# A fused decoder layer: the transfers that keep u's low half, and one more pair by seven products

## The chip, the cores and the metric

The kernel runs on one core of a Trainium2 chip. A core has five engines with an instruction queue each, every queue strictly in order: TensorE (PE, matrix products into PSUM banks), VectorE (DVE), ScalarE (ACT), GpSimd (POOL) and SyncE (SP). ACT, POOL and SP also issue DMA transfers, in the order in which they stand in their queues. The metric is the device time of one execution in microseconds (us).

## The reference, cut to what matters

One decoder layer on 256 tokens of width 2048, in fp32. The attention half (two head groups of eight heads) is not touched. The second half is

```python
h = rmsnorm(x, norm_mlp_pre)
u = square(relu(h @ w_up))            # w_up 2048 x 8192
x = x + rmsnorm(u @ w_down, norm_mlp_post)   # w_down 8192 x 2048
```

## The kernel before, in words

**Products.** A fp32 number is split in two rounded halves, hi = round(a) and lo = a - hi. A product then is three matmuls into one PSUM bank (hi by hi, hi by lo, lo by hi; line 296, called by `three`). A weight tile of 128 rows by 1024 columns (`raw`) is loaded by SP, ACT rounds it to `hi` (line 306, or 310 with a row gain) and DVE subtracts to get `lo` (307 or 311). There are five `raw` buffers and eight of `hi` and `lo`; ACT and DVE may work up to six tiles ahead of PE.

**Seven products.** Two weight tiles and two 128-row blocks of the left operand form a 2 by 2 block product, which eight products do plainly. For some pairs it is done by seven (Strassen's way, `seven_products`): 21 matmuls for 24. Such a pair is loaded by one POOL DMA of 1024 KB (line 374); DVE makes the sums `t` and `u` of weights (lines 361, 365, 366), and half a tile and three whole ones are split in place of two. Extra sums are gathered in four more banks `m` and added at the end (`close`, lines 1052 and 1055, and 1121).

**Up projection.** Eight chunks j of 1024 columns. Chunks 2 to 5 do rows 8 to 15 tile by tile (8 tiles) and rows 0 to 7 as four pairs by seven. The pairs are loaded by turns into the buffers `ab` and `ab2`; the profile and the queue listings print `ab2` as `ab` too, the listings with a number (`ab_3503`). A buffer may be loaded again once DVE has made the last `lo` from it. At a chunk's end DVE adds the extra sums (1121), ACT makes relu with the row scale (937, tile `r`), PE transposes `r` (line 300, tile `rt`), and ACT squares that into u (949). The first transposes of a chunk stand among the matmuls of the next chunk, and PE can pass nothing that waits. Between the first and the second `r`, ACT's queue holds a `hi<-u` that needs the next chunk's first weight sums.

**u's low half.** u has 16 pieces g of 128 by 1024, two per chunk. Its low half is made by DMAs rather than by DVE (`lo_away`): for each 512-column half ACT writes minus the rounded u into a tile `neg` (line 960; it shares the two buffers of tag `r`), ACT's queue sends it to `ukeep` in DRAM (962), and a POOL DMA with an addition adds u to it (964), for which POOL's queue waits until the first transfer has landed. The down projection loads the result back as `ulo` (976), and ACT makes `uhi` (975).

**Down projection.** Two halves c of 1024 output columns, each over 16 pieces g, that is 32 pairs kp, of which `DOWN_SEVEN` lists those by seven. Left sums of u for a pair are made and split by DVE and ACT (989 to 991, tile `s`). For a pair in both lists the first half stores `s` in DRAM (983, on SP) and the second half loads it (404, on POOL).

**What sets the order.** The program is laid down once, by a planner with a clock of its own (`Flow`). Each matmul moves the clock by 0.216 planned us. Side work is a generator: `flow.start(gen, d)` starts it d planned us later, `yield d` puts its next step d planned us on, and a step's instructions are appended to their engines' queues at that point. Weight tiles are emitted when PE's plan is within the look-ahead.

Of the kernel before, what the change touches and what calls it, by code (L numbers as in the profile page):

```python
# [101 lines left out]
def up_steps(first, *groups):  # L102
    steps = [("k", k) for k in first]
    for i, ks in enumerate(groups):
# [9 lines left out]
N_SEVEN = [sum(w == "w" for w, _ in steps) for steps in UP_STEPS]  # L114


DOWN_SEVEN = ((5, 7, 9, 11, 15, 17, 19, 21, 25, 27, 29), range(3, 28, 2))
SHARED = [k for k in DOWN_SEVEN[0] if k in DOWN_SEVEN[1]]
GT = FF // 512
DOWN_STEPS = [[s for kp in range(2 * GT)  # L120
               for s in ([("w", kp)] if kp in ws else [("k", 2 * kp), ("k", 2 * kp + 1)])] for ws in DOWN_SEVEN]

# [141 lines left out]
def layer(nc, tc, io):  # L264
    flow = Flow()
# [12 lines left out]
    def bank(i, name):  # L278
        return ps.tile([P, 512], F32, tag=f"bank{i}", bufs=1, name=name)
# [19 lines left out]
    def transpose(out, a):  # L299
        nc.tensor.transpose(out, a, ident)  # L300
        flow.spend(TR)
# [128 lines left out]
    def seven_down(c, kp):  # L430
        def load():

            n = DOWN_SEVEN[c].index(kp)
            raw = dpl["ab"]
# [498 lines left out]
    def up_evac(j, b, i, acc, order):  # L933

        yield UP_STEP * order
        r = late["up"].tile([P, 512], F32, tag="r", bufs=2, name=f"r{j}_{b}")
        nc.scalar.activation(r, acc, AF.Relu, scale=rstd2[b])
        yield D_UP if j > 1 else 2 * D_UP
        t = bank(i, f"rt{j}_{b}")
        for k in range(4):  # L940
            transpose(t[:, k * P:(k + 1) * P], r[:, k * P:(k + 1) * P])
        if j not in uT:
            if j in (0, 1, 10, 11, 12, 13):
                t2 = late["u01" if j < 2 else "ab2" if j < 12 else "ab"][:, j % 2 * CW:(j % 2 + 1) * CW]
            else:
                tag = {"tag": "T", "bufs": 2} if j > 13 else {}
                t2 = late["up"].tile([P, CW], F32, name=f"uT{j}", **tag)
            uT[j] = t2.rearrange("p (k s) -> p k s", k=4)
        nc.scalar.activation(uT[j][:, :, b * P:(b + 1) * P], t.rearrange("p (k s) -> p k s", k=4), AF.Square)
        if b and j:  # L950
            flow.start(lo_away(j), 5.0 + 7.0 * (j % 2))

    def lo_away(g):

        ukeep[g] = dram.tile([P, CW], F32, name=f"ukeep{g}")
        u = uT[g].rearrange("p k s -> p (k s)")
        for h in range(2):
            c = slice(h * 512, (h + 1) * 512)
            t = late["up"].tile([P, 512], F32, tag="r", bufs=2, name=f"neg{g}_{h}")
            nc.scalar.activation(t.bitcast(F32R), u[:, c], AF.Copy, scale=-1.0)  # L960
            yield 1.0
            nc.scalar.dma_start(out=ukeep[g][:, c], in_=t)
            yield 9.0
            nc.gpsimd.dma_start(out=ukeep[g][:, c], in_=u[:, c], accum_op=OP.add)
            yield 2.0

# [96 lines left out]
    for j in range(FF // CW):  # L1063
# [9 lines left out]
        for t, b in order:  # L1073
# [19 lines left out]
            if what == "k":  # L1093
                w = weights.get(tiles[0])
                h_done(k, b)
                for n in range(2):
                    c = slice(n * 512, (n + 1) * 512)
                    three(accs[b, n], [tok(hT[x], k, b) for x in range(2)], [w[x][:, 0, c] for x in range(2)], t == 0, t == len(steps) - 1)
                    if j == 0 and t == len(steps) - 1:
                        evac.append(flow.start(up_evac(n, b, at[b, n], accs[b, n], 2 * b + n - 0.25 * (2 * b + n))))  # L1100
                    flow.pump()
                if b == NB - 1:
                    weights.free(tiles[0])
                continue
# [13 lines left out]
        if j:  # L1118

            for bn in PARTS:  # L1120
                nc.vector.tensor_tensor(out=accs[bn], in0=accs[bn], in1=more[bn], op=OP.add)
            for o, (b, n) in enumerate(PARTS):
                evac.append(flow.start(up_evac(2 * j + n, b, at[b, n], accs[b, n], o + 0.6)))
# [85 lines left out]
    for c in range(2):  # L1209
# [3 lines left out]
        accs = {(b, n): y[b][2 * c + n] for b, n in PARTS}  # L1213
        ws = DOWN_SEVEN[c]
        for t, (what, k, tiles) in enumerate(wide_d[c]):
# [102 lines left out]
```

## Time and profile before

| what | value |
|---|---|
| median of 3 runs | 1054.12 us (1051.59 to 1059.64) |
| the profiled execution's own time | 1057.15 us |
| its span (first to last instruction) | 1055.2 us |
| granted TensorE clock | 0.997 |
| PE busy | 1035.3 us, 98% |
| DVE busy | 834.4 us, 79% |
| ACT busy | 645.3 us, 61% |
| POOL busy | 90.0 us, 9% |

The up projection lies at about 354 to 711 us of the span, the down projection's first half at 711 to 871, its second half from there to 1047. A matmul's shown duration (about 389 ns) overlaps the next one's, so a busy PE is read by the distance of starts. In rows of the trace, `x <-y` is output and input, `[n <-E z]` is the idle time of the engine just before, and what ended it. Waits give a total, a count and the longest. Line numbers are those of the kernel before.

### The profile page before, as it was taken

The page shows a single profiled execution, that of the slowest core. Times are in us where ns is not written, and L with a number is a line of the kernel's source. Part 1 is how long each engine was busy: PE and PEld are TensorE (multiplying, and loading weights), DVE is VectorE, ACT ScalarE, POOL GpSimd, SP SyncE. Part 2 cuts the span into 40 slices and gives each one's busy share as a digit, 9 for nine tenths or more (in the row PEclk, how much of TensorE's full clock was granted, in tenths as well). Part 3 has the DMA queues.
Part 4 walks back from the last instruction along what each step waited for, and adds up shares of the span by engine and source line. Part 5 has one row for each costly group of instructions (what it writes and reads, how often), then busy time and mean ns, then how long its engine had stood idle before and what let it go on. Part 6 is the DMA issues. An engine that isn't in the chain of part 4 may idle for free.

```text
span 1055.2 us, 13457 instructions
## 1 busy us (share of the span) xinstructions
PE 1035.3 (98%) x4828; PEld 859.5 (81%) x4828; DVE 834.4 (79%) x1122; ACT 645.3 (61%) x884; POOL 90.0 (9%) x134
## 2 busy tenths in 40 slices
PE   9999999999999999999999999899999999999996
PEld 6888899888888788888877778787888888888885
DVE  6776546577556679998989889788889888998895
ACT  6675436566454567576756667667666664867661
POOL 0000000000000000111110111011110101111100
PEclk9999999999999999999999999999999999999998
DMA  9974546454356295758778687589997977789872
GB/s 303 369 232 147 147 131 222 145 175 152 129 197 221 86 374 160 242 169 287 221 235 251 201 249 196 189 273 353 305 333 271 358 251 244 287 302 344 339 240 80
DMA packets 89395, 248.21 MB, mean 235 GB/s; under 512 B 7920, under 2 KB 12528, under 8 KB 88944
## 3 DMA queue, kind: packets, MB, share of 16 engines
q1 hardware_dynamic: 61984, 162.03, 45.3%
q0 software_dynamic: 22592, 77.08, 23.4%
q10 hardware_dynamic: 4752, 8.24, 2.1%
q8 instruction: 38, 0.62, 0.2%
q14 instruction: 29, 0.24, 0.1%
HBM read 222.16 MB, written 25.17 MB: 234 GB/s over the span
## 4 chain that ended last, share of the span: by engine, by line
PE 78%; DVE 10%; DMA 6%; issue 3%; ACT 2%; POOL 0%; ACTq 0%; DVEq 0%; SPq 0%; POOLq 0%
PE y L296 24%; PE acc_u L296 11%; PE acc_o L296 8%; PE md L296 6%; PE acc_qk L296 4%; PE acc_v L296 4%; DVE lo L307 3%; PE m L296 3%; PE acc_ckv L296 2%; DVE lo L311 2%; DMA raw<-in_w_up 2%; PE acc_ukv L296 2%; PE acc_q L296 2%; PE acc_cq L296 2%; PE acc_k L296 2%
## 5 line engine op out<-in xcount | busy, mean ns | idle before, releaser
L307 DVE TENSOR_TENSOR lo<-raw,hi 128x1024 fp32r<-128x1024 f32 (+3 forms) x207 | 233.8, 1150 | 81.8 <-ACT hi L306 80.7
L306 ACT ACTIVATE hi<-raw 128x1024 fp32r<-128x1024 f32 (+3 forms) x207 | 203.4, 997 | 69.3 <-DMA raw<-in_w_in 14.4
L296 PE MATMUL acc_u<-hi,hT_hi 128*128 128x512 f32 x356 | 142.0, 399 | 0.4 <-DVE c L1055 0.4
L296 PE MATMUL acc_u<-hi,hT_lo 128*128 128x512 f32 x356 | 139.2, 391 | 0.4 <-DVE hT_lo L307 0.4
L296 PE MATMUL acc_u<-lo,hT_hi 128*128 128x512 f32 x356 | 138.8, 390 | 0.0
L296 PE MATMUL y<-hi,uhi 128*128 128x512 f32 x352 | 137.3, 390 | 0.0
L296 PE MATMUL y<-hi,ulo 128*128 128x512 f32 x352 | 137.0, 389 | 0.0
L296 PE MATMUL y<-lo,uhi 128*128 128x512 f32 x352 | 136.9, 389 | 0.0
L311 DVE SCALAR_TENSOR_TENSOR lo<-raw,gcol,hi 128x1024 fp32r<-128x1024 f32 x74 | 92.6, 1279 | 12.7 <-ACT hi L310 12.7
L310 ACT ACTIVATE hi<-raw,gcol 128x1024 fp32r<-128x1024 f32 x74 | 82.9, 1145 | 27.8 <-DMA raw<-in_w_up 21.1
L296 PEld LDWEIGHTS acc_u<-hi,hT_lo 128*128 128x128 f32 x356 | 66.8, 188 | 15.2 <-DVE hT_lo L307 0.8
L296 PEld LDWEIGHTS acc_u<-hi,hT_hi 128*128 128x128 f32 x356 | 66.9, 188 | 14.1 <-DVE c L1055 1.4
L296 PEld LDWEIGHTS acc_u<-lo,hT_hi 128*128 128x128 f32 x356 | 67.0, 188 | 12.7
L296 PEld LDWEIGHTS y<-lo,uhi 128*128 128x128 f32 x352 | 66.1, 188 | 13.7
L296 PEld LDWEIGHTS y<-hi,ulo 128*128 128x128 f32 x352 | 66.1, 188 | 13.7
L296 PEld LDWEIGHTS y<-hi,uhi 128*128 128x128 f32 x352 | 66.1, 188 | 13.6
L306 ACT ACTIVATE hi<-u 128x1024 fp32r<-128x1024 f32 (+1 forms) x38 | 37.6, 991 | 61.1 <-DVE u L366 47.4
L307 DVE TENSOR_TENSOR lo<-st_down,hi 128x1024 fp32r<-128x1024 f32 x48 | 57.6, 1220 | 1.5 <-ACT hi L306 1.5
L306 ACT ACTIVATE hi<-st_down 128x1024 fp32r<-128x1024 f32 x48 | 50.0, 1050 | 3.5 <-DVE st_down L366 1.1
L296 PE MATMUL md<-hi,s 128*128 128x512 f32 x144 | 52.1, 389 | 0.0
L296 PE MATMUL acc_o<-hi,mixT_hi 128*128 128x512 f32 x128 | 51.8, 405 | 0.0
L296 PE MATMUL acc_o<-hi,mixT_lo 128*128 128x512 f32 x128 | 50.2, 392 | 0.0
(330 smaller groups left out, 2167.9 us busy)
## 6 DMA issues: line engine op xcount, KB each, us to landing
raw<-in_w_down SPq DMA_DIRECT2D x80, 512.0 KB, 6.4
raw<-in_w_up SPq DMA_DIRECT2D x76, 512.0 KB, 5.8
raw<-in_w_in SPq DMA_DIRECT2D x55, 512.0 KB, 4.9
ab<-in_w_up POOLq DMA_DIRECT2D x22, 1024.0 KB, 8.0
raw<-in_w_out SPq DMA_DIRECT2D x32, 512.0 KB, 4.4
ulo<-ukeep POOLq DMA_DIRECT2D x30, 512.0 KB, 6.2
ab_down<-in_w_down POOLq DMA_DIRECT2D x13, 1024.0 KB, 9.4
ukeep<-neg ACTq DMA_DIRECT2D x30, 256.0 KB, 5.5
```

What stands on the lines that cost most here:

```text
L296: nc.tensor.matmul(out, a, b, start=start, stop=stop)
L306: nc.scalar.activation(hi, src, AF.Copy)
L307: nc.vector.tensor_tensor(out=lo, in0=src, in1=hi.bitcast(F32), op=OP.subtract)
L310: nc.scalar.activation(hi, src, AF.Copy, scale=g)
L311: nc.vector.scalar_tensor_tensor(out=lo, in0=src, scalar=g, in1=hi.bitcast(F32), op0=OP.mult, op1=OP.subtract)
```

## The change

Two things are changed. In `lo_away`, the two `neg` steps of a piece stand 8 planned us apart and begin 2 or 6 us after u is complete (before: 12 apart, beginning at 5 or 12), and both adding DMAs come after them, 31 and 25 planned us after their own `neg` was sent (before: 9), two together. In the down projection's first half, pairs 13 and 23 go by seven and pair 17 does not: twelve pairs for eleven, of which eleven rather than ten are shared with the second half.

```diff
-DOWN_SEVEN = ((5, 7, 9, 11, 15, 17, 19, 21, 25, 27, 29), range(3, 28, 2))
+DOWN_SEVEN = ((5, 7, 9, 11, 13, 15, 19, 21, 23, 25, 27, 29), range(3, 28, 2))
...
         if b and j:
-            flow.start(lo_away(j), 5.0 + 7.0 * (j % 2))
+            flow.start(lo_away(j), 2.0 + 4.0 * (j % 2))
...
             yield 1.0
             nc.scalar.dma_start(out=ukeep[g][:, c], in_=t)
-            yield 9.0
+            yield 7.0
+        yield 16.0
+        for h in range(2):
+            c = slice(h * 512, (h + 1) * 512)
             nc.gpsimd.dma_start(out=ukeep[g][:, c], in_=u[:, c], accum_op=OP.add)
             yield 2.0
```

POOL's queue before, during chunk 3 (pieces 4 and 5 are written away): first the load of its last pair, then the next chunk's first three (`ab_3503` is `ab2`; `ukeep_4589` and `ukeep_4672` are pieces 4 and 5).

```order
L374 DMA ab_3503<-in_w_up 128x2x1024
L964 DMA ukeep_4589<-uT_4485 128x512
L964 DMA ukeep_4672<-uT_4505 128x512
L374 DMA ab<-in_w_up 128x2x1024
L964 DMA ukeep_4589<-uT_4485 128x512
L964 DMA ukeep_4672<-uT_4505 128x512
L374 DMA ab_3503<-in_w_up 128x2x1024
L374 DMA ab<-in_w_up 128x2x1024
```

The same place after the change, where `ukeep_4553` and `ukeep_4621` are pieces 4 and 5.

```order
L374 DMA ab_3503<-in_w_up 128x2x1024
L374 DMA ab<-in_w_up 128x2x1024
L967 DMA ukeep_4553<-uT_4483 128x512 x2
L374 DMA ab_3503<-in_w_up 128x2x1024
L967 DMA ukeep_4621<-uT_4503 128x512 x2
L374 DMA ab<-in_w_up 128x2x1024
```

The next chunk's first load has nothing between it and the load ahead of it; its second load stands behind two additions of piece 4 rather than behind four of pieces 4 and 5, and its third behind piece 5's.

ACT's queue before, in chunk 3, from the first halves of `neg` on.

```order
L960 ACTIVATE neg_0_4590<-uT_4485 128x512
L310 ACTIVATE hi_4600<-raw_4598,gcol 128x1024
L962 DMA ukeep_4589<-neg_0_4590 128x512
L306 ACTIVATE hi_4611<-ab 128x512
L306 ACTIVATE hi_4627<-ab 128x1024
L306 ACTIVATE hi_4634<-u_2_4594 128x1024
L306 ACTIVATE hi_4644<-t_2_4593 128x1024
L310 ACTIVATE hi_4662<-raw_4660,gcol 128x1024
L960 ACTIVATE neg_0_4673<-uT_4505 128x512
L306 ACTIVATE hi_4675<-ab_3503 128x512
L962 DMA ukeep_4672<-neg_0_4673 128x512
```

After the change, from the same piece's first half on.

```order
L960 ACTIVATE neg_0_4554<-uT_4483 128x512
L306 ACTIVATE hi_4560<-ab_3503 128x512
L306 ACTIVATE hi_4564<-ab_3503 128x1024
L306 ACTIVATE hi_4572<-u_1_4518 128x1024
L962 DMA ukeep_4553<-neg_0_4554 128x512
L306 ACTIVATE hi_4583<-t_1_4517 128x1024
L310 ACTIVATE hi_4601<-raw_4599,gcol 128x1024
L306 ACTIVATE hi_4611<-ab 128x512
L960 ACTIVATE neg_0_4622<-uT_4503 128x512
L962 DMA ukeep_4621<-neg_0_4622 128x512
L306 ACTIVATE hi_4631<-ab 128x1024
L306 ACTIVATE hi_4638<-u_2_4595 128x1024
```

The first `neg` stands ahead of the second pair's four `hi` rather than behind them, and the second piece's `neg` comes within the third pair rather than the fourth. The list of DVE's instructions in the up projection is the same in both kernels.

DVE's queue in the down projection's first half after pair 11's splits, before: piece 6 has no pair by seven, and two plain tiles follow before the left sums of pair 15 (`uT_4890`).

```order
L307 TENSOR_TENSOR lo_6844<-st_down,hi_6843 128x1024
L307 TENSOR_TENSOR lo_6854<-st_down,hi_6853 128x1024
L307 TENSOR_TENSOR lo_6868<-raw_6865,hi_6867 128x1024
L307 TENSOR_TENSOR lo_6890<-raw_6887,hi_6889 128x1024
L989 TENSOR_TENSOR st_down<-uT_4890 128x256
L990 TENSOR_TENSOR st_down<-st_down,uT_4890 128x128
L991 TENSOR_TENSOR st_down<-uT_4890,st_down 128x128
```

After the change the same stretch holds pair 13's left sums (tile `s_13`) and its weight sums.

```order
L992 TENSOR_TENSOR st_down<-uT_4868 128x256
L993 TENSOR_TENSOR st_down<-st_down,uT_4868 128x128
L994 TENSOR_TENSOR st_down<-uT_4868,st_down 128x128
L307 TENSOR_TENSOR lo_6845<-st_down,hi_6844 128x1024
L307 TENSOR_TENSOR s_13_6854<-st_down,s_13_6854 128x512
L307 TENSOR_TENSOR lo_6858<-st_down,hi_6857 128x1024
L361 TENSOR_TENSOR st_down<-ab_down 128x1024
```

Pieces 2 to 7 and 9 to 14 now have a pair by seven, two runs of six; before, the runs were pieces 2 to 5, 7 to 10 and 12 to 14.

## The prediction

> **What bounds the kernel now.** I read the page first, then PE's waits, then the engines in order of time around each wait, then the chain behind them. The page:
>
> ```profile
> PE 1035.3 (98%) x4828; PEld 859.5 (81%) x4828; DVE 834.4 (79%) x1122; ACT 645.3 (61%) x884; POOL 90.0 (9%) x134
> ```
>
> PE sets the time, so a gain is either a matmul less or a stall of PE less. PE's waits between 450 and 730 us (total, times, longest):
>
> ```profile
> PE rt L300 <- ACT r L937: 9.2, 6, 1.8
> PE acc_u L296 <- DVE c L1055: 0.4, 1, 0.4
> ```
>
> That is the up projection's whole loss: 9.6 us. In order of time, the bracket giving PE's idle time:
>
> ```profile
> 538.48 0.66 PE L300 MATMUL rt<-ident,r 128*128 128x128 f32 x4 [1.25 <-ACT r L937]
> 576.72 0.51 PE L296 MATMUL acc_u<-hi,hT_hi 128*128 128x512 f32 x1 [0.43 <-DVE c L1055]
> 584.02 0.66 PE L300 MATMUL rt<-ident,r 128*128 128x128 f32 x4 [1.77 <-ACT r L937]
> 628.93 0.66 PE L300 MATMUL rt<-ident,r 128*128 128x128 f32 x4 [1.76 <-ACT r L937]
> 670.77 0.66 PE L300 MATMUL rt<-ident,r 128*128 128x128 f32 x4 [1.41 <-ACT r L937]
> 677.43 0.66 PE L300 MATMUL rt<-ident,r 128*128 128x128 f32 x4 [1.40 <-ACT r L937]
> 720.08 0.66 PE L300 MATMUL rt<-ident,r 128*128 128x128 f32 x4 [1.57 <-ACT r L937]
> ```
>
> All stand at the ends of chunks (sum 9.59). ACT's `r` waits there for DVE's closing additions, so DVE is late. Why, DVE's order of time shows: once a chunk it waits for the load of a pair.
>
> ```profile
> 498.88 1.23 DVE L361 TENSOR_TENSOR t<-ab 128x1024 f32<-128x1024 f32 x1 [2.30 <-DMA ab<-in_w_up]
> 543.70 1.23 DVE L361 TENSOR_TENSOR t<-ab 128x1024 f32<-128x1024 f32 x1 [2.58 <-DMA ab<-in_w_up]
> 589.34 1.23 DVE L361 TENSOR_TENSOR t<-ab 128x1024 f32<-128x1024 f32 x1 [2.68 <-DMA ab<-in_w_up]
> 633.83 1.23 DVE L361 TENSOR_TENSOR t<-ab 128x1024 f32<-128x1024 f32 x1 [2.26 <-DMA ab<-in_w_up]
> ```
>
> The chain of waits (start, length) says why that load is late:
>
> ```profile
> 482.55 6.92 DMA ukeep<-neg
> 489.51 0.46 issue
> 489.99 0.54 POOL ukeep L964
> 490.53 8.26 DMA ab<-in_w_up
> ```
>
> The load stands in POOL's queue behind an addition that waits for its `neg` to land. One chunk on, DVE's last read of the buffer `ab2` and POOL's queue, with what POOL waited for:
>
> ```profile
> 518.26 1.82 DVE L307 TENSOR_TENSOR lo<-ab,hi 128x512 fp32r<-128x512 f32 x2
> 517.77 1.05 POOL L374 DMA_DIRECT2D ab<-in_w_up  x1
> 526.34 0.86 POOL L964 DMA_DIRECT2D ukeep<-uT  x1 [7.52 <-DMA ukeep<-neg]
> 534.67 0.87 POOL L964 DMA_DIRECT2D ukeep<-uT  x1 [7.47 <-DMA ukeep<-neg]
> 535.21 1.07 POOL L374 DMA_DIRECT2D ab<-in_w_up  x1
> ```
>
> The buffer is free at 518.26 + 1.82 = 520.1, the load goes out at 535.2: 15.1 us lost.
>
> **The additions.** After the change only two additions of the even piece stand before that load, and their `neg` tiles were written within the second and third pair of the chunk. ACT's rows there before, where `hi<-u` is the last thing ahead of, first, the sending of the first `neg`, and second, the making of the next (the order after the change):
>
> ```profile
> 501.65 1.06 ACT L306 ACTIVATE hi<-u 128x1024 fp32r<-128x1024 f32 x1 [0.26 <-DVE u L366]
> 509.45 1.06 ACT L306 ACTIVATE hi<-u 128x1024 fp32r<-128x1024 f32 x1 [2.75 <-DVE u L366]
> DMA to landing us min/median/max: 2.0/5.5/8.3
> ```
>
> The last row is the landing of all `neg` transfers. The even piece's second half is sent about 2 us after 509.45 + 1.06, once `neg` (0.6) and a `hi` (1.0) are done, at 512.5, and lands by 518.0, at the longest 520.8. The buffer is free at 520.1, so the load can go out 15 us earlier, against a wait of 2.3 to 2.7: the wait goes with some 12 us to spare. The odd piece's additions, now behind this load, hold up only the chunk's third load, whose buffer comes free a pair later. The cover for the two `neg` is the 7.8 us between the rows quoted: the second needs the first one's buffer, so the longest landing (8.3) would hold ACT by 0.5, out of the 2.75 it idles there. ACT's work and DVE's order are the same.
>
> What is late next? From one chunk's closing additions to the next:
>
> ```profile
> 531.64 2.49 DVE acc_u L1121 x4
> 577.17 2.49 DVE acc_u L1121 x4
> ```
>
> That is 45.53 us for DVE, of which PE stalled 0.43 + 1.77 = 2.20, so PE needs 43.3. DVE without its 2.58 needs 42.95: PE becomes the slower by 0.4.
>
> Per boundary I set the DVE wait saved against PE's stall: 2.30 against 1.25, 2.58 against 2.20, 2.68 against 1.76, 2.26 against 2.81 (1.41 + 1.40), nothing against 1.57. If DVE's lead is carried from chunk to chunk the surplus (1.05 + 0.38 + 0.92 = 2.35) covers the last two as well, and 9.59 goes. If none is carried, 1.25 + 2.20 + 1.76 + 2.26 = 7.47 goes. The eight `hi`/`lo` buffers limit a lead, by how much no row shows; I take the middle, 8.5.
>
> Against that stand the weight tiles of SP, which must now land beside the earlier pair load:
>
> ```profile
> 563.18 7.79 DMA raw<-in_w_up
> 572.26 1.28 DVE L311 SCALAR_TENSOR_TENSOR lo<-raw,gcol,hi 128x1024 fp32r<-128x1024 f32 x1 [0.31 <-ACT hi L310]
> 658.47 8.34 DMA raw<-in_w_up
> 668.10 1.28 DVE L311 SCALAR_TENSOR_TENSOR lo<-raw,gcol,hi 128x1024 fp32r<-128x1024 f32 x1 [2.21 <-ACT hi L310]
> 520.00:525.00 5.00, 5.00 (x23) 4.13 (x22) 5.00 (x6) 4.01 (x5) 0.00 (x0) 1.00 0.96 334
> ```
>
> A landing of 7.79 cost DVE 0.31, one of 8.34 cost 2.21 at a shorter distance. The window's last two numbers, DMA share 0.96 and 334 GB/s, show that the stretch of 520 is full already. But the load of 517.77 moves out of it (to about 512, when its buffer is free and no addition is ahead) as the load of 535.21 moves in: the bytes beside the tiles stay about the same. I take 0.5 us lost in all, with 0 and 2.2 as ends.
>
> [...]
>
> **The pairs by seven.** One pair more in the first half: 21 matmuls for 24. From the chain, from ACT and DVE in the run of pieces 7 to 10, and the page's window there:
>
> ```profile
> 746.90 5.44 PE y L296 x24
> 801.49 1.22 DVE L361 TENSOR_TENSOR st_down<-ab_down 128x1024 f32<-128x1024 f32 x1
> 812.12 1.22 DVE L361 TENSOR_TENSOR st_down<-c 128x1024 f32<-128x1024 f32 x1
> 821.73 1.07 ACT L306 ACTIVATE hi<-raw 128x1024 fp32r<-128x1024 f32 x1 [1.07 <-PE y L296]
> 800.00:850.00 50.00, 50.00 (x222) 41.42 (x221) 45.73 (x55) 31.88 (x36) 4.82 (x8) 1.00 0.85 306
> ```
>
> A matmul takes 5.44 / 24 = 0.227, three less save 0.68. PE has no stall in this window (50.00 of 50). A piece with such a pair takes DVE 812.12 - 801.49 = 10.63 and PE 45 x 0.227 = 10.2; DVE falls behind 0.43 a piece. After a run of four, ACT still waits 1.07 for PE to free a buffer, so DVE is at its full lead; two more pieces cost 0.86 of it, which the lead covers. Without cover, the two longer runs would cost up to 4 x 0.43 = 1.7, more than the 0.68. In the second half pair 17's left sums replace those of 13 and 23 on DVE; one more 512 KB store (SP) and one more load (POOL) go beside work that never stalls PE. I count them at nothing.
>
> **The sum.** -8.5 + 0.5 - 0.68 = -8.7 us. The profiled execution would go from 1057.15 (its span of 1055.2 and 1.95 around it) to 1048.5. The median shown is 3.0 lower than it; stalls and matmuls are the same in every execution, so I take the same off the median: 1054.12 - 8.7 = 1045.4.
>
> **Rivals.**
> - *Only the first three boundaries recover.* The last two hang on tiles landing late (2.21 above), and no lead is carried. Then 1.25 + 2.20 + 1.76 + 0.68 = 5.9: 1048.2. For it: the 8.34. Against: the 2.26 in that same chunk goes too.
> - *The load was not what DVE lacked.* Something just as late takes its place, an ACT `hi` say, and the stalls stay: only 0.68, 1053.4. Against: DVE's 42.95 against PE's 43.3.
> - *Slower: the tiles take the place of the pairs.* In every chunk the earlier load lands in the full stretch of 520 and slows the tile at 563. Upper bound for a landing is the slowest group of loads, `c` in the down projection:
>
> ```profile
> c<-in_w_down POOLq DMA_DIRECT2D x5, 1024.0 KB, 12.1
> ```
>
> At 12.1 for 7.79 DVE loses 4.3 a chunk and saves 2.46 (the mean of the four); 1.85 later, six boundaries: +11.1 - 0.68 = +10.4, 1064.5. It decides from a landing of 7.79 + 2.46 = 10.2 on. Against: the other load moves out of the stretch. [...]
>
> **How the numbers follow.** Forecast 0.65, first rival 0.15, second 0.13, slower 0.07. The forecast's own range: with 9.59 + 0.68 = 10.3 gone 1043.9, with 7.47 + 0.68 - 2.2 = 5.9 gone 1048.2. For 8 in 10 I take both other gains in and 1.9 for the scatter of a median below: 1042 to 1054. About 1%, 10.5 us, is what a measurement of this kernel tells from no change. The forecast's best end (10.3) just misses it, so faster by over 1% is only a matter of scatter at that end: 0.22. Slower by over 1% is half of the last rival: 0.04. Within: 0.74.
>
> **What would show it.** Right: DVE's waits for `ab` between 450 and 730 gone, POOL's second load of a chunk going out right after the buffer's last `lo`, PE's waits for `r` under 2 us in all, three matmuls fewer, no wait of PE in the down projection. Wrong: ACT waiting longer for `raw` in each chunk (third rival) or for a `neg` to land, DVE waiting at the same place for something else, or PE stalls in pieces 6, 7, 13 and 14 of the first half.

## The result, and the profile after

The changed kernel takes 1052.38 us (median of 20 runs, 1049.68 to 1055.18), the kernel before on the same chip 1057.79 us (20 runs, 1051.59 to 1061.6). The ratio is 0.9955, with an interval of 0.9943 to 0.9967: 4.8 us less, between 3.5 and 6.0. Forecast were 8.7 us less and a time of 1045.4. The time lies inside the range (1042 to 1054), near its upper end; "within 1%" came true.

The profiled execution of the changed kernel took 1050.85 us (span 1049.1, granted clock 0.998). The engines' line of its page, and PE's waits from 440 to 1040 us (total, times, longest):

```profile
PE 1035.0 (99%) x4825; PEld 859.4 (82%) x4825; DVE 838.2 (80%) x1127; ACT 644.5 (61%) x886; POOL 91.4 (9%) x136
PE rt L300 <- ACT r L937: 2.0, 4, 1.4
PE y L296 <- DVE lo L307: 1.8, 1, 1.8
```

Three matmuls fewer (4825 for 4828). The up projection's loss has gone from 9.6 us to 2.0, but a wait that the kernel before did not have stands in the down projection. PE's waits in order of time:

```profile
538.23 0.66 PE L300 MATMUL rt<-ident,r 128*128 128x128 f32 x4 [0.23 <-ACT r L937]
664.58 0.66 PE L300 MATMUL rt<-ident,r 128*128 128x128 f32 x4 [0.21 <-ACT r L937]
671.23 0.66 PE L300 MATMUL rt<-ident,r 128*128 128x128 f32 x4 [1.37 <-ACT r L937]
712.54 0.66 PE L300 MATMUL rt<-ident,r 128*128 128x128 f32 x4 [0.22 <-ACT r L937]
896.37 0.50 PE L296 MATMUL y<-lo,uhi 128*128 128x512 f32 x1 [1.77 <-DVE lo L307]
```

The row at 896 lies early in the down projection's second half, right behind its first pair by seven, and just after the first half's results have been added up (line 1193 after the change, on DVE from 878 to 891). Below, "the start of the second half" means this place. One boundary of the up projection kept its stall: the row at 671.23 stands 6.65 us behind the one at 664.58, as 677.43 stood 6.66 behind 670.77 before, so it is the second of that boundary's two. POOL's queue where the load lost 15 us before:

```profile
512.04 0.72 POOL L374 DMA_DIRECT2D ab<-in_w_up  x1 [7.04 <-DVE lo L307]
512.76 0.95 POOL L967 DMA_DIRECT2D ukeep<-uT  x1
515.47 0.87 POOL L967 DMA_DIRECT2D ukeep<-uT  x1 [1.76 <-DMA ukeep<-neg]
519.84 0.74 POOL L374 DMA_DIRECT2D ab<-in_w_up  x1 [3.50 <-DVE lo L307]
```

The second load of the chunk goes out at 519.84 (535.21 before), and what released it is DVE's last read of its buffer. DVE's waits from 440 to 720 us have no row for a load of a pair any more (four of 2.3 to 2.7 us before); the two longest in total are:

```profile
DVE lo L307 <- ACT hi L306: 9.6, 18, 1.6
DVE lo L311 <- ACT hi L310: 2.8, 2, 2.6
```

Where the new wait comes from can be read from the same few instructions in both traces: SP's issue of a weight tile near the end of the first half, and the moment at which PE gave ACT a `hi` buffer free there (ACT's wait of 1.66, the same step in both). The third row is ACT's `hi` of that tile, once it has landed; the last row of the changed kernel sums SP's waits from 845 to 875. The kernel before, then the changed one:

```profile
863.29 0.33 SPq L190 DMA_DIRECT2D raw<-in_w_down  x1
865.93 2.01 ACT L306 ACTIVATE hi<-raw 128x1024 fp32r<-128x1024 f32 x2 [1.66 <-PE y L296]
869.24 1.06 ACT L306 ACTIVATE hi<-raw 128x1024 fp32r<-128x1024 f32 x1 [1.30 <-DMA raw<-in_w_down]
```

```profile
856.33 0.33 SPq L190 DMA_DIRECT2D raw<-in_w_down  x1
857.69 1.07 ACT L306 ACTIVATE hi<-raw 128x1024 fp32r<-128x1024 f32 x1 [1.66 <-PE y L296]
863.24 1.06 ACT L306 ACTIVATE hi<-raw 128x1024 fp32r<-128x1024 f32 x1 [2.96 <-DMA raw<-in_w_down]
864.34 1.23 DVE L307 TENSOR_TENSOR lo<-raw,hi 128x1024 fp32r<-128x1024 f32 x1 [2.79 <-ACT hi L306]
SPq L190 <- DVE lo L307: 27.5, 10, 9.1
```

Measured against PE's progress, the tile was issued 2.64 us ahead before (865.93 - 863.29) and 1.36 us ahead after: 1.28 us later. The last run of pieces with a pair by seven was three long and is now six; three pieces more, at 0.43 us of lag each, are 1.29. SP's load waits for a `raw` buffer, and it is DVE that releases one, by its `lo` (ten waits here). So DVE's lag reaches SP's queue although ACT still finds all eight `hi` buffers full at 857.69. The tile then lands late, DVE waits 2.79 us for ACT's `hi` of it, and DVE has the closing of the first half yet to do before the `lo` that PE wants at 896.

The lag is one of two parts. Measured against PE, ACT's `hi` of the tile comes 2.24 us later than before (5.55 behind ACT's wait for PE rather than 3.31): 1.28 us from the issue, the other 0.96 from a landing of 6.81 us rather than 5.85. The lead of the issue is the same in all executions, those of the experiments below included, that end the half with the same run: 1.33 to 1.36 us in the seven with six pieces, 2.64 or 2.65 in the ten with three. The landing scatters, from 5.4 to 8.0 us. In nine of the eleven executions with a wait of PE for `lo` at this place, the wait is the landing less the lead less 3.7 us. (The kernel with thirteen pairs is left out of these counts, and that with the later adding up of the eleven.)

### The profile page after: what moved, and what is told of

Its sections match the earlier page's. It is cut to its first block, busy times and chain, and to the rows that moved or that the text cites. A ratio compares the mean times of both kernels' runs of the same rounds, so it can differ in the third digit from the quotient of the medians.

```text
span 1049.1 us, 13455 instructions
## 1 busy us (share of the span) xinstructions
PE 1035.0 (99%) x4825; PEld 859.4 (82%) x4825; DVE 838.2 (80%) x1127; ACT 644.5 (61%) x886; POOL 91.4 (9%) x136
## 4 chain that ended last, share of the span: by engine, by line
PE 84%; DVE 10%; issue 2%; ACT 2%; DMA 1%; POOL 0%; DVEq 0%; POOLq 0%; ACTq 0%
PE acc_u L296 20%; PE y L296 18%; PE acc_o L296 8%; PE m L296 6%; PE md L296 5%; DVE lo L307 4%; PE acc_qk L296 4%; PE acc_v L296 4%; PE acc_ckv L296 2%; PE acc_ukv L296 2%; PE acc_q L296 2%; PE acc_cq L296 2%; PE acc_k L296 2%; PE acc_uq L296 2%; PE rt L300 1%
## 5 line engine op out<-in xcount | busy, mean ns | idle before, releaser
L307 DVE TENSOR_TENSOR lo<-raw,hi 128x1024 fp32r<-128x1024 f32 (+3 forms) x205 | 231.2, 1148 | 83.2 <-ACT hi L306 82.5
L296 PE MATMUL y<-lo,uhi 128*128 128x512 f32 x346 | 134.7, 389 | 1.8 <-DVE lo L307 1.8
L296 PE MATMUL y<-hi,uhi 128*128 128x512 f32 x346 | 135.0, 390 | 0.0
L296 PE MATMUL y<-hi,ulo 128*128 128x512 f32 x346 | 134.7, 389 | 0.0
L296 PEld LDWEIGHTS acc_u<-hi,hT_lo 128*128 128x128 f32 x356 | 66.8, 188 | 15.1 <-DVE hT_lo L307 0.9
L307 DVE TENSOR_TENSOR lo<-st_down,hi 128x1024 fp32r<-128x1024 f32 x50 | 60.0, 1218 | 1.0 <-ACT hi L306 1.0
L296 PE MATMUL md<-hi,s 128*128 128x512 f32 x150 | 54.3, 389 | 0.0
```

What stands on the lines that cost most here:

```text
L296: nc.tensor.matmul(out, a, b, start=start, stop=stop)
L307: nc.vector.tensor_tensor(out=lo, in0=src, in1=hi.bitcast(F32), op=OP.subtract)
```

## The experiments

Times are medians; a ratio is against the kernel before, run on the same chip beside it. What is compared is compared there.

### The whole change again, and each part alone

First the changed kernel once more, unaltered.

> The changed kernel once more, as the yardstick for the runs beside it. Both theories: 4 to 6.5 us under the kernel before; PE's waits for r in the up projection about 2 us in all, and one wait of PE of about 1.8 us for a lo at the start of the down projection's second half.

1051.87 us, ratio 0.9926 (0.9902 to 0.9949): by the ratio 7.8 us less, more than the 4 to 6.5 expected. PE waits 1.41 us for `r` (at 670.20) and 1.25 us (1.8 expected) at the start of the second half.

The transfers alone, with the list of pairs of before:

```diff
-DOWN_SEVEN = ((5, 7, 9, 11, 13, 15, 19, 21, 23, 25, 27, 29), range(3, 28, 2))
+DOWN_SEVEN = ((5, 7, 9, 11, 15, 17, 19, 21, 25, 27, 29), range(3, 28, 2))
```

> Only the neg steps and the additions are moved; the pairs by seven are as before (last run of pieces with a pair: 12 to 14). Theory A (lag: in a run of pieces with a pair DVE loses 0.43 us a piece, the loads of weight tiles are released by DVE, and the lag arrives at the start of the second half): the 1.8 us wait there is gone, the up projection's stalls are at 2 us as in the changed kernel, so 7.6 us under the kernel before and about 1.1 (1.8 - 0.68) under the changed kernel. Theory B (shift: the stall comes from the down projection's transfers meeting others once the up projection ends sooner): a wait of 1 us or more stays there, and the time is 0.7 above the changed kernel.

1050.37 us, ratio 0.9913 (0.9891 to 0.9934). The up projection waits the same 1.4 us, and the second half starts with 0.68 us:

```profile
895.55 0.50 PE L296 MATMUL y<-lo,uhi 128*128 128x512 f32 x1 [0.68 <-DVE lo L307]
```

The wait is shorter, as theory A had it, but not gone. The first part alone is at least as fast as the whole, with three matmuls more. The pairs alone, with the transfers of before (an edit of the kernel before):

```diff
-DOWN_SEVEN = ((5, 7, 9, 11, 15, 17, 19, 21, 25, 27, 29), range(3, 28, 2))
+DOWN_SEVEN = ((5, 7, 9, 11, 13, 15, 19, 21, 23, 25, 27, 29), range(3, 28, 2))
```

> Only the pairs are changed; neg and additions are as before. Theory A: the up projection's 9.6 us of stalls stay, and PE waits 1 to 2 us for a lo at the start of the second half, so 0.3 to 1.3 us slower than before. Theory B: no such wait, 0.7 us faster than before.

1057.51 us, ratio 0.9998 (0.9975 to 1.0021): no gain, though 0.68 us of matmuls are gone. PE's waits for `r`, and its wait at the start of the second half:

```profile
PE rt L300 <- ACT r L937: 6.2, 3, 2.6
903.80 0.50 PE L296 MATMUL y<-lo,uhi 128*128 128x512 f32 x1 [1.92 <-DVE lo L307]
```

So the longer wait belongs to the pairs and comes with the old up projection too. The rows also show something that the prediction had ruled out: with transfers as before, this execution lost 7.0 us in the up projection (6.2 and 0.8 for other sums) and not 9.6.

### How long the runs of pieces are

Still twelve pairs, but pair 17 by seven and pair 23 not: runs of nine pieces (2 to 10) and three (12 to 14) in place of two of six.

```diff
-DOWN_SEVEN = ((5, 7, 9, 11, 13, 15, 19, 21, 23, 25, 27, 29), range(3, 28, 2))
+DOWN_SEVEN = ((5, 7, 9, 11, 13, 15, 17, 19, 21, 25, 27, 29), range(3, 28, 2))
```

> The changed kernel with pair 17 by seven instead of pair 23: twelve pairs as well, in runs of nine pieces (2 to 10) and three (12 to 14) instead of six and six. Theory A: the lag at the start of the second half is that of three pieces, so the 1.8 us wait there is under 0.6, and the time is 1.2 to 1.8 under the changed kernel; a wait of PE in or behind the run of nine (3.9 us lost) would say that the lead of DVE is shorter than that. Theory B: the wait stays at 1.8 and the time is that of the changed kernel.

1050.22 us, ratio 0.9921 (0.9896 to 0.9946). PE has one wait over 0.2 us from 440 us to the end, that at 670; none at the start of the second half. The tile's issue, and the same step of ACT:

```profile
854.96 0.33 SPq L190 DMA_DIRECT2D raw<-in_w_down  x1
857.61 1.06 ACT L306 ACTIVATE hi<-raw 128x1024 fp32r<-128x1024 f32 x1 [1.65 <-PE y L296]
```

2.65 us ahead of PE again, as before the change: what counts is the run that ends the half. Then thirteen pairs, pieces 2 to 14 without a break:

```diff
-DOWN_SEVEN = ((5, 7, 9, 11, 13, 15, 19, 21, 23, 25, 27, 29), range(3, 28, 2))
+DOWN_SEVEN = ((5, 7, 9, 11, 13, 15, 17, 19, 21, 23, 25, 27, 29), range(3, 28, 2))
```

> The changed kernel with pair 17 by seven as well: thirteen pairs in the first half, pieces 2 to 14 without a break in place of two runs of six. Three matmuls fewer (0.68 us). Theory A (DVE falls 0.43 us behind in each piece with such a pair, and the weight tiles that its late releases bring in late make PE wait at the start of the second half): the lag of seven more pieces (3.0) comes on top of the 1.25 to 1.77 us, so far as PE does not wait earlier, inside the run: 3 to 5 us of PE's waits for lo in and after the first half; 1 to 3 us slower than the changed kernel. Rival B (that wait comes from the earlier end of the up projection, not from the runs): it stays at 0.7 to 1.8 us, and the time is 0.7 lower than the changed kernel's.

1053.94 us, ratio 0.9975 (0.9954 to 0.9995): by the ratios slower than the changed kernel, as theory A said and B did not, though the two weren't run beside each other and the intervals just meet. But the waits at the start of the second half sum to 2.6 us (0.38, 0.20 and the row below), not to the 3 to 5 that seven more pieces were to give. The lag does not pile up without end; where the rest of it goes no run shows. What follows the wait costs almost as much. PE's row, and a window behind it (PE's busy time, then the granted clock, DMA share and GB/s):

```profile
898.73 0.50 PE L296 MATMUL y<-lo,uhi 128*128 128x512 f32 x1 [2.06 <-DVE lo L307]
899.30:902.30 3.00, 3.00 (x8) 0.50 0.97 376
```

After the wait the clock is halved from 899.2 to 902.6 us. The first 30 matmuls behind the wait take 8.55 us; behind the 1.77 of the changed kernel's first profile, where the clock stays, they take 6.94: 1.6 us more.

The last of this group starts the adding up of the first half's results 6 planned us later:

```diff
-            h_evac = flow.start(half_evac(more, g_half))
+            h_evac = flow.start(half_evac(more, g_half), 6.0)
```

> The changed kernel, with the adding up and evacuation of the first half's results (four additions of 0.62 us and one of 0.69 on DVE, the squares on ACT) started 6 planned us later in the second half. Theory A (PE's wait of 1.25 to 1.77 us there is DVE's work: DVE comes late out of its run, and the evacuation stands ahead of the tile that PE lacks): 3.2 us of DVE's work go behind that tile and the wait goes (0 to 0.3 us); PE could wait for a bank of the first half instead, which would show as a wait of y for y. Rival (the wait is a weight tile's landing, 6.8 us from a late issue, whatever DVE does in between): 1.2 us or more of it stay.

1054.98 us, ratio 0.997 (0.9952 to 0.9989). The wait for `lo` is gone, but PE now waits for banks of the first half, twice and ahead of that place:

```profile
893.34 0.50 PE L296 MATMUL md<-hi,s 128*128 128x512 f32 x1 [2.21 <-DVE c L1197]
897.88 0.50 PE L296 MATMUL md<-hi,s 128*128 128x512 f32 x1 [2.20 <-DVE c L1197]
```

This does not decide between the two theories: a PE that is held up 2.2 us at 893 would not have met a wait of 1.3 to 1.8 at 895 in any case, and banks whose adding up starts later come free later whether or not DVE lacks time. A sixth `raw` buffer, the direct trial of the reading, was not tried.

### Which half of the first part does it

Only the additions later, the pieces of `neg` at their old start and distance, the pairs of before. (The two additions stand 27 and 17 planned us behind the sending of their own piece; the 31 and 19 of the expectation are miscounted.)

```diff
-            yield 9.0
+            yield 11.0
+        yield 4.0
+        for h in range(2):
+            c = slice(h * 512, (h + 1) * 512)
             nc.gpsimd.dma_start(out=ukeep[g][:, c], in_=u[:, c], accum_op=OP.add)
```

> Only the additions are queued later (31 and 19 planned us after their own piece was sent, both together); the two pieces of minus u keep their old start (5 or 12) and distance (12), and the pairs by seven are those of before. In POOL's queue the load that lost 15 us then has no addition ahead of it whose piece is still on its way. Theory (the order of POOL's queue is the whole cause, the closeness of the pieces is not): PE's waits for r at 1.4 to 2.2 us as with the whole first part, DVE's waits for a pair's load under 1 us, ratio to before 0.990 to 0.994. Rival (the pieces must also be closer, or the additions still meet a transfer that has not landed): POOL waits for a landing ahead of a load, DVE's waits for the load stay at 2 us or more a chunk, ratio 0.997 to 1.000.

1048.74 us (1048.02 to 1049.36), ratio 0.9915 (0.9886 to 0.9944). PE's waits from 440 to 1040 us, and POOL's queue:

```profile
PE y L296 <- DMA ulo<-ukeep: 0.8, 1, 0.8
PE rt L300 <- ACT r L937: 0.3, 1, 0.3
523.22 0.88 POOL L967 DMA_DIRECT2D ukeep<-uT  x1 [9.28 <-DMA ukeep<-neg]
523.79 1.04 POOL L374 DMA_DIRECT2D ab<-in_w_up  x1
```

Here an addition does wait, 9.28 us, ahead of the chunk's second load, which goes out at 523.79 rather than 519.84. That is early enough: DVE has no wait for a pair, and the up projection loses 0.3 us, less than the 1.4 to 2.2 expected. Now the reverse: pieces earlier and closer as in the change, but each addition 5 planned us after its own piece:

```diff
-            flow.start(lo_away(j), 5.0 + 7.0 * (j % 2))
+            flow.start(lo_away(j), 2.0 + 4.0 * (j % 2))
...
-            yield 9.0
+            yield 5.0
```

> Only the pieces of minus u stand earlier and closer (start 2 or 6, 8 apart); each addition is queued 5 planned us after its own piece was sent, one at a time as before, so that additions stand ahead of the third and fourth load of a chunk with their piece still on its way. Pairs by seven as before. Theory (what counts is that no addition waits ahead of the load whose buffer has long been free): the loads of the next chunk's first pairs go out at once, PE's waits for r fall to 1.4 to 3 us; the additions now wait for landings of 5.5 us ahead of a load whose buffer is only then free, which costs DVE under 1 us a chunk; ratio 0.990 to 0.995. Rival (any addition that waits for a landing in POOL's queue costs the load behind it, wherever it stands): DVE waits 2 us or more for the pair behind it, once a chunk, and the stalls of 7 to 10 us stay; ratio 0.997 to 1.000.

1058.11 us, ratio 1.0003 (0.9973 to 1.0034): by the time the rival held, but PE's waits for `r` come to 4.4 us, not to 7 to 10. They, POOL's queue, the load in the chain of waits, and a wait of DVE:

```profile
PE rt L300 <- ACT r L937: 4.4, 5, 2.0
522.06 0.86 POOL L964 DMA_DIRECT2D ukeep<-uT  x1 [4.68 <-DMA ukeep<-neg]
522.61 1.78 POOL L374 DMA_DIRECT2D ab<-in_w_up  x2
522.61 9.59 DMA ab<-in_w_up
532.98 0.69 DVE L307 TENSOR_TENSOR lo<-ab,hi 128x512 fp32r<-128x512 f32 x1 [1.97 <-ACT hi L306]
```

Additions that wait one by one hold the queue until two loads go out together at 522.6, and the first of them takes 9.59 us to land. DVE waits only 0.8 us in all for a pair's load itself; here the late load holds up ACT, and DVE waits 1.97 us for ACT's `hi` of it. The rest of the time lies elsewhere: PE waits 3.1 us in the down projection of this execution, and its clock drops behind the longest wait for `r` (0.83 on the mean from 540 to 550 us, see the last section). So the closer pieces bring no time by themselves, and the later additions are the whole gain; that each execution loses the same time in the same place doesn't follow.

### The stall that stayed at 670 us

It is in all executions of the changed kernel and of its variants above, at 1.37 to 1.41 us. Its size can be read from ACT's `hi` of the last chunk's first weight tile. In the changed kernel:

```profile
660.72 1.15 ACT L310 ACTIVATE hi<-raw,gcol 128x1024 fp32r<-128x1024 f32 x1 [5.87 <-DMA raw<-in_w_up]
```

PE's transposes follow 10.51 us later (671.23 - 660.72). What PE has left to do until then decides the stall, and that tile's landing decides when the 10.51 start. In that window the changed kernel sends four additions back to back (POOL, 649.4 to 653.0). Taken apart by giving chunk 5's pieces, written away just there, their old place in the changed kernel:

```diff
-            flow.start(lo_away(j), 2.0 + 4.0 * (j % 2))
+            flow.start(lo_away(j), 5.0 + 7.0 * (j % 2) if j in (10, 11) else 2.0 + 4.0 * (j % 2))
...
-            yield 7.0
-        yield 16.0
+            yield 11.0 if g in (10, 11) else 7.0
+        yield 4.0 if g in (10, 11) else 16.0
```

> The changed kernel, but the pieces of minus u that belong to chunk 5 alone (written away during chunk 6) stand at their old start and distance (5 or 12, 12 apart), so that their four additions go out one to ten us apart rather than back to back; the rest of the changed order, POOL's queue included, stays. Theory C (the last stall of the up projection, 1.4 us at 670 to 671 us, comes from the four additions that the changed kernel sends back to back into the window in which the last chunk's first weight tile must land): ACT's wait for that tile falls from 5.9 to 3 us or less, the stall of 1.4 us goes to 0.3 or less, and the time is about 1.3 us under the changed kernel's. Rival (the stall comes from DVE being late after six chunks, and the additions are beside the point): it stays at 1.2 to 1.5 us.

1052.29 us, ratio 0.9955 (0.9936 to 0.9974); the stall is still 1.26 us, again 10.51 us behind the tile:

```profile
659.70 1.15 ACT L310 ACTIVATE hi<-raw,gcol 128x1024 fp32r<-128x1024 f32 x1 [4.27 <-DMA raw<-in_w_up]
670.21 0.66 PE L300 MATMUL rt<-ident,r 128*128 128x128 f32 x4 [1.26 <-ACT r L937]
```

The wait for the tile fell only to 4.27 us rather than to 3, and the stall stayed, so this execution speaks against the theory of the four additions. The mirror image was run later: additions later and nothing else, but the closer pieces for chunk 5 only (as an edit of the kernel with the additions alone):

```diff
-            flow.start(lo_away(j), 5.0 + 7.0 * (j % 2))
+            flow.start(lo_away(j), 2.0 + 4.0 * (j % 2) if j in (10, 11) else 5.0 + 7.0 * (j % 2))
...
-            yield 11.0
-        yield 4.0
+            yield 7.0 if g in (10, 11) else 11.0
+        yield 16.0 if g in (10, 11) else 4.0
```

> Additions queued later, pairs by seven as before, and the closer, earlier pieces of minus u for chunk 5 alone (written away during chunk 6); those of all other chunks stand as before. If the four additions of chunk 5, sent back to back, make the last chunk's first weight tile land late (theory C, which the mirror image did not bear out), the stall at 670 us is back with 1.2 us or more. If it hangs on the pieces of the earlier chunks, it stays at 0 to 0.5 us. If it is scatter of a landing in single executions, it may be anything in between, and the times tell nothing.

1049.04 us, ratio 0.993 (0.9909 to 0.9952), and the stall is back with 1.40 us. An earlier wait of DVE, SP's issue of the tile, ACT's `hi` of it, and the stall:

```profile
629.44 0.69 DVE L307 TENSOR_TENSOR lo<-ab,hi 128x512 fp32r<-128x512 f32 x1 [0.64 <-ACT hi L306]
650.63 0.33 SPq L190 DMA_DIRECT2D raw<-in_w_up  x1
659.53 1.15 ACT L310 ACTIVATE hi<-raw,gcol 128x1024 fp32r<-128x1024 f32 x1 [5.92 <-DMA raw<-in_w_up]
670.04 0.66 PE L300 MATMUL rt<-ident,r 128*128 128x128 f32 x4 [1.40 <-ACT r L937]
```

So in this execution chunk 5's closer pieces were enough to make it. Over all executions: with them closer, 1.37 to 1.41 us (eight executions); at the old distance with the additions later, 0, 0.26, 0.49, 0.65, 0.91 and 1.26 (six). The closer pieces cost about 0.8 us here on the mean; at the old distance the stall scatters with the tile's landing, and the 1.26 was at its upper end. The traces of these fourteen take it apart in part. The tile is issued 0.28 to 0.31 us ahead of ACT's last wait for PE in all eight with the pieces closer, 0.82 us ahead in all six with them at the old distance: 0.5 us later, and 20 us before, well ahead of the four additions, the eight have a wait of DVE for ACT's `hi` (0.64 in the row at 629.44, 0.28 to 0.30 in the others) that the six lack. That part belongs to ACT's changed order. The rest is the landing, 8.3 to 8.8 us in the eight and 7.2 to 8.7 in the six; whether the additions' traffic lengthens it was not tried.

### What each piece is worth, side by side

Additions later and the change's twelve pairs (this edit and the next are of the kernel with the additions alone):

```diff
-DOWN_SEVEN = ((5, 7, 9, 11, 15, 17, 19, 21, 25, 27, 29), range(3, 28, 2))
+DOWN_SEVEN = ((5, 7, 9, 11, 13, 15, 19, 21, 23, 25, 27, 29), range(3, 28, 2))
```

> Additions queued later, pieces of minus u as before (5 or 12, 12 apart), and the changed kernel's list of pairs (two runs of six pieces). Theory A: against the kernel with the additions alone, 0.68 us less matmuls and 1.2 to 1.9 us of PE's wait for lo at the start of the second half more: 0.5 to 1.2 us slower, ratio to before 0.991 to 0.993. Rival (the runs cost nothing here): no wait there, 0.7 us faster.

1050.66 us, ratio 0.9938 (0.9916 to 0.9961). The wait of the longer run is there, and again the clock falls behind it (0.66 is its mean in this window):

```profile
895.12 0.68 PE L296 MATMUL y<-lo,uhi 128*128 128x512 f32 x1 [2.05 <-DVE lo L307]
895.00:900.00 5.00, 4.88 (x14) 0.66 0.94 344
```

Additions later and pair 17 in place of 23:

```diff
-DOWN_SEVEN = ((5, 7, 9, 11, 15, 17, 19, 21, 25, 27, 29), range(3, 28, 2))
+DOWN_SEVEN = ((5, 7, 9, 11, 13, 15, 17, 19, 21, 25, 27, 29), range(3, 28, 2))
```

> Additions queued later, pieces of minus u as before, and pair 17 rather than 23 among the twelve pairs (runs of nine pieces and of three). From the runs so far: PE's waits in the up projection under 0.5 us, none at the start of the second half (the last run is short), three matmuls fewer than with the additions alone: 0.7 us under that kernel, ratio 0.990 to 0.991, the fastest of all. Rival (the longer first run costs in the first half): PE waits there and the 0.7 us are not seen.

1048.39 us, ratio 0.993 (0.9907 to 0.9952), on the chip of the 1050.66: 2.3 us under it. The only wait of PE over 0.2 us between 440 us and the end is one of 0.26. Both ratios lie above what was expected (0.991 to 0.993, and 0.990 to 0.991). Three versions were then run once more beside each other on one chip: the additions alone, those with pair 17, and the changed kernel.

> The kernel with the additions alone queued later, once more, on one chip with the changed kernel and with the version of pair 17. Expected from its first runs: PE's waits for r under 0.5 us, 1.5 to 3 us faster than the changed kernel, ratio to before 0.990 to 0.993. If the closer pieces are no loss, it is within 1 us of the changed kernel.

> Additions queued later and pair 17 rather than 23, once more, on the same chip. Expected: 0.7 us (three matmuls) faster than with the additions alone, no wait at the start of the second half, ratio to before 0.989 to 0.992. If the list of twelve pairs brings nothing, both are the same within 0.3 us.

> The changed kernel a third time, as the measure for the three others on this chip: ratio to before 0.992 to 0.996, PE's wait at the start of the second half 1.2 to 2.0 us.

| version | median, us | ratio to before (interval) |
|---|---|---|
| the changed kernel | 1052.19 | 0.9955 (0.9939 to 0.9971) |
| additions later alone | 1048.44 | 0.9926 (0.9904 to 0.9949) |
| additions later, pair 17 | 1048.35 | 0.9922 (0.99 to 0.9944) |

Both versions beat both kernels, by some 3.8 us the changed one (1.5 to 3 were expected of the additions alone); pair 17's 0.68 us can't be told here (its execution had a wait of 0.71 at the start of the second half). The changed kernel's own profile shows why it lags: PE's wait there and a window behind it, at half clock:

```profile
897.43 0.50 PE L296 MATMUL y<-lo,uhi 128*128 128x512 f32 x1 [2.06 <-DVE lo L307]
899.00:902.00 3.00, 3.00 (x9) 0.50 0.92 351
```

Last, the kernel before for one more profile:

> The kernel before, unchanged, for another profiled execution: whether the up projection's stalls, which the prediction took as 9.59 us in every execution, vary. Seen so far: 9.6 in the first profile, 7.0 in the execution that changed only the pairs. Expected: PE's waits for r and for the weight sums between 6.5 and 10 us in all; a span that follows them.

1059.67 us. PE's waits in the up projection are three of these four rows, 8.7 us:

```profile
PE rt L300 <- ACT r L937: 7.7, 5, 2.1
PE y L296 <- DVE lo L307: 1.0, 1, 1.0
PE acc_u L296 <- DVE c L1055: 0.8, 2, 0.4
PE acc_u L296 <- ACT c L1052: 0.2, 1, 0.2
```

With the 9.6 of the first profile and the 7.0 of the pairs alone, the old order loses 8.4 us on average, and the start of the second half already costs it 1.0 us in some executions.

## Why the prediction was right or wrong

**The cause of the stalls: right.** The load behind an addition that waits for its `neg` was what DVE lacked: with the additions behind it, the load went out at 519.84 as DVE freed the buffer, DVE's waits for a pair vanished, and the sign "PE's waits for `r` under 2 us in all" was met within a rounding (2.0, then 1.4 twice). All fourteen executions with the additions later are without a wait of DVE for a pair's load from 440 to 720 us. Both sides were tried: additions alone give the whole gain, closer pieces none. Of the two moves in that part the prediction did not ask which one it needed; its argument (a `neg` landing by 518.0) leaned on the closer ones, which the runs show to be a loss of about 0.8 us on the mean at the end of chunk 6.

**The size of the first term: nearly right, but of one execution.** -8.5 + 0.5 was to go; 9.59 - 2.03 = 7.6 went, and 8.2 in the two later executions of the changed kernel (1.4 left). The step that failed is "stalls and matmuls are the same in every execution". The order of before lost 7.0 (in the kernel with the pairs alone), 8.7 and 9.6 us; the profile used was at the upper end. Against the mean of 8.4 and 1.6 left, the term is -6.8. The split over the boundaries was half right: the first three, that at 670.77 and that at 720.08 recovered; the one at 677.43 kept its 1.4 (671.23 after the change). It stands 10.5 us behind ACT's `hi` of the tile that the prediction quotes with 8.34 and 2.21, and what that `hi` waited for, 5.87 us, was the tile's landing and not DVE.

**The pairs: the sign failed.** The step "two more pieces cost 0.86 of it, which the lead covers" miscounted the run that matters: the last one goes from three pieces to six, three more, not two. And it looked at the eight `hi` and `lo` buffers. Those did cover: ACT still waited for PE to free one, and no wait came in pieces 6, 7, 13 or 14. What the step left out are the five `raw` buffers, which DVE releases: a late DVE means a late issue of the next tiles, 1.28 us for three more pieces in the last run, as the per-piece lag of 0.43 says. It also asked for the slack in the middle of the half, where PE has none of its waits, rather than at its end, where DVE also has the closing additions to make. The new wait is 1.25, 1.77 and 2.3 us (2.06 and 0.20) in three executions of the changed kernel, 0 and 0.99 in two of the old: about 1.3 us more, as much as the tile's issue lost of its lead; the scatter is that of its landing. The price without cover had been put at up to 1.7, which holds this mean; it was not in the sum.

**The sum, remade.** -6.8 - 0.68 + 1.3 = -6.2 us. Measured were 4.8, 7.8 and 4.8 us less by the three ratios (0.9955, 0.9926 and 0.9955 of about 1058). Where the wait was 2.06 us (the third execution), the clock's drop behind it took 1.6 us more, which no term had. Of the 38 timed executions of the changed kernel 12 had a mean clock of 0.996 or less; in the first series those lie about 2 us above the ones of 0.998 (medians of seven at 1053.2 and of ten at 1051.2). But so had 18 of the 80 executions of the kernel before that ran beside the experiments, so the change adds only about (0.32 - 0.23) x 2 = 0.2 us by it. That makes -6.0: inside the second and third interval (5.4 to 10.4 and 3.1 to 6.4 us less) and at the edge of the first (3.5 to 6.0).

**The absolute time: the base failed too.** The 1054.12 was the median of three runs; twenty gave 1057.79. Of the 7.0 us between forecast and result 3.7 are the base, 3.3 the change.

**The rivals.** The first (only some boundaries recover) gave 5.9 us less, near the sum remade, and is half right by its own reason: the stall behind the late tile (677.43) stayed. Those at 670.77 and 720.08 went, and the rest of the missing gain lay in the down projection. The second fell: the load was what DVE lacked. The third fell as well: the pair loads, now early, landed faster and not slower, and DVE's only wait for a tile's `hi` before that late tile was one of 0.2 us. The median landing (last number, us) of the 22 loads, before and after:

```profile
ab<-in_w_up POOLq DMA_DIRECT2D x22, 1024.0 KB, 8.0
ab<-in_w_up POOLq DMA_DIRECT2D x22, 1024.0 KB, 6.0
```

The weight tiles of the up projection went from a median of 5.8 to 6.4 us. What of the 2.0 us that were left is due to this, the term put at 0.5, no run separates.

## What to carry to other kernels

In POOL's queue here, DMAs that had to wait for another transfer (7.52 and 7.47 us) held up the load queued behind them by 15.1 us, so queue such a DMA behind the load whose buffer will be free first; moving the waiting one alone was enough (ratio 0.9915), and moving what it waits for earlier brought nothing (1.0003). When an engine is allowed to fall behind on the strength of a lead, count every pool of buffers that it releases, those of the loads too, and look for the loss at the end of the stretch, where the engine meets its next burst of work. A sum made on one profiled execution inherits that execution's stalls: look at two or three before taking a stall's size as a constant.

## What the runs showed of the hardware that was not expected

In three executions a wait of PE of 2.05 or 2.06 us cost nearly twice, 1.6 us more. The granted clock stayed at 1.00 behind all waits under 2 us, the 1.92 at 903.80 among them, and behind this one of 2.00 in the kernel with chunk 5's pieces at their old place:

```profile
895.93 0.50 PE L296 MATMUL y<-lo,uhi 128*128 128x512 f32 x1 [2.00 <-DVE lo L307]
896.00:899.00 3.00, 3.00 (x13) 1.00 0.89 320
```

It fell behind waits of 2.05, 2.06 and 2.06 at that place, as quoted above, behind the second of the two of 2.2 (not behind the first), and in the up projection behind one of 2.00 (at 540.43, the closer pieces alone) and one of 2.63 (at 718.23, the pairs alone). In all six it falls to half (0.50 in the windows of 3 us behind the two of 2.06), 0.1 to 1.5 us after PE has started again, and stays there for 3.4 us (in windows of 10 us, what the clock lacks to 1.00 sums to 1.7 us behind each of the six, half of 3.4). Behind the 2.05 and the two of 2.06 the next 30 matmuls take 8.54 to 8.56 us rather than the 6.94 or 6.95 behind the shorter waits at that place: 1.6 us. So in these executions the drops came behind waits of 2.00 to 2.63 us, but not behind every such wait: 2.00 and 2.2 are on both sides, and one of 2.12 in the kernel before (at 720.98) drew no drop. What sets them apart no run shows. No window of 10 us between 440 and 1030 us shows a clock under 0.995 without such a wait, in any kernel. The scatter of times fits this: in 24 timed executions of the versions without a wait over 1 us (additions later, with the pairs of before or pair 17) the mean clock never was under 0.997, and their times lie within 1046.7 to 1050.8.
